# The triangular inverse of a Gated-DeltaNet layer: one stretch of products per doubling step instead of two

## The chip, the cores and the metric

The kernel runs on one core of a Trainium2 chip. The metric is the device time of one launch in microseconds, taken as the median of several runs. Four compute engines matter here: PE (TensorE, the matrix array), DVE (VectorE), ACT (ScalarE) and POOL (GpSimd). SP's queue issues the loads from HBM.

## The reference, cut to what matters

The program is a two-layer trunk for 512 tokens of width 1024. Each layer has a mixer and a gated MLP with a short convolution. Layer 0 mixes by four mLSTM heads and four Gated-DeltaNet heads; layer 1 by HGRN2. The change is in the Gated DeltaNet:

```python
def gated_delta_chunkwise(q, k, v, g, beta):
    ...
    kk = jnp.einsum("nbhld,nbhsd->nbhls", kc, kc)
    a_mat = jnp.where(strict, bc[..., :, None] * kk * decay, 0.0) + jnp.eye(L)
    rhs = jnp.concatenate([vc * bc[..., None], kc * (bc * jnp.exp(G))[..., None]], -1)
    sol = lax.linalg.triangular_solve(a_mat, rhs, left_side=True, lower=True, unit_diagonal=True)
    u, w = sol[..., :DV], sol[..., DV:]
```

Every chunk of every head needs the inverse of a unit lower triangular matrix, I plus a strictly lower part. Everything is float32.

## The kernel before, in words

**Tiles.** The kernel takes chunks of P = 128 tokens, so the 512 tokens are NT = 4 chunks. The four Gated-DeltaNet heads are done two at a time: `gdn_pair` is called once for pair 0 and once for pair 1, and each call has PC = 8 matrices of 128x128 to invert (two heads, `a` = 0 and 1, of four chunks). The matrix sits transposed and negated in `mt`, made on DVE from products of k with itself and the decay `dec`.

**The inverse.** A 128x128 matrix is cut in two diagonal blocks of 64 rows, one in partitions 0 to 63 (`lo`) and one in 64 to 127 (`hi`). For the 16 such blocks of a pair, the kernel keeps the inverse X of the block diagonal part found so far and its transpose, in tiles `X` and `xt` of 128 partitions x 8 x 64. They begin as identities (`units`). The step of level b (2, 4, 8, 16, 32) doubles the size of the blocks from b to 2b:
- 16 products `pp` = X times M (L1184), each 64x64, into one PSUM bank;
- ACT copies that bank to SBUF, into `PR` (L1186);
- 16 products `pe` (L1190) and 16 `pet` (L1191), which multiply `PR` by X from the other side, as they are and transposed, into two banks;
- on DVE, `fill` (L1100, a copy_predicated) takes from `pe` what the mask of the level lets through into `X`, and the same from `pet` into `xt`, with the masks `masks` and `maskst`.

Level 1 needs no product but a turn of the matrix into place (`pp` at L1155 and `pq` at L1156), and the end joins the two 64-row blocks (L1197, L1200, L1205) and has ACT copy the result into `mt` (L1209, L1210). Between the levels the program has the products of k and q (`at`, ahead of level 2), the transposes of q (`qt`, ahead of level 8, whose squares ACT sums into `nq`) and of v (`vt`, ahead of levels 16 and 32).

**What stands around it.** The weights are split into a high and a low part: ACT casts a loaded weight to `whi` (L228), and DVE or POOL subtracts to get `wlo` (L99). A projection of 128x512 is then three products (L127, `uh`/`ul` with `whi`/`wlo`), named `pf` for the short convolution's inputs and `pt` for a 256 columns wide one. Such products are independent of the inverse, and they are set between its stretches on PE. The convolution itself is a row of `scalar_tensor_tensor` on DVE (L102), and its silu is on ACT. `gdn(0)`, `mlstm(0)`, `gdn(1)` and `mlstm(1)` are written in this order, and a scheduler interleaves their instructions by the tiles that they need; `issue_after` pins one instruction behind another. What comes out is one order for each engine, in which the engine waits at each instruction until its inputs are there.

**PSUM.** Eight banks: three for projections, two (`mxt`) that the products of the inverse take in turn, two named "sc", one named "po".

Of the kernel before, what the change touches and what calls it, by code (L numbers as in the profile page):

```python
# [18 lines left out]
P = 128  # L19
# [15 lines left out]
def kernel(  # L35
# [741 lines left out]
    def ab_mix(pm, u, x0, g0):  # L777
# [7 lines left out]
        def small(name, shape, bufs=1, dt=F32):  # L785
            return pm.tile(shape, dt, tag=name, name=name, bufs=bufs)
# [27 lines left out]
        then(A.activation, out=one, in_=one, func=AF.Sqrt)  # L814
        unit = [units(then)]

# [150 lines left out]
        mk = small("masks", [P, 5, 64 // 4], dt=I32)  # L967
        mkt = small("maskst", [P, 6, 32 // 4], dt=I32)
        for i, hf in enumerate((slice(0, 64), slice(64, P))):
            nc.sync.dma_start(  # L970
                out=mk[hf],
                in_=block_masks[hf, P // 4 : 6 * P // 4].rearrange("p (l n) -> p l n", l=5)[:, :, i * 16 : (i + 1) * 16],
            )
            for j in range(len(RADIX4)):
                at = (6 + 3 * j) * P // 4
                nc.sync.dma_start(
                    out=mkt[hf, 2 * j : 2 * j + 2],
                    in_=block_masks[hf, at : at + P // 2].rearrange("p (l n) -> p l n", l=2)[:, :, i * 8 : (i + 1) * 8],
                )
        mk, mkt = mk.bitcast(U8), mkt.bitcast(U8)  # L980
        th = small("th", [P, NT, 8])
# [105 lines left out]

        def fill(b, x_, data, t):

            def part(ap):  # L1090
                return ap.rearrange("p c (n a r) -> p c n a r", a=2, r=b)[:, :, :, t, :]

            if t:
                mask = mkt[:, LEVELS.index(b), :].rearrange("p (n r) -> p n r", r=b)
            elif b == 1:
# [3 lines left out]
            mask = mask.unsqueeze(1).broadcast_to([P, PC, 32 // b, b])  # L1099
            V.copy_predicated(out=part(x_), mask=mask, data=part(data))  # L1100

        def gdn_pair(j, k, q, vf, gates):
            heads = (2 * j, 2 * j + 1)
            decs, qds, kbes, kds, pts = ([None, None] for _ in range(5))
            gl = small("gl", [P, 2, NT], bufs=2)
            ss = col(8, "l2s")
            for a, h in enumerate(heads):
# [11 lines left out]
                tt(V, v4(kd), v4(pt), bc(v4(dec)[:, :, P - 1], P), ALU.mult)  # L1119
                decs[a], qds[a], kbes[a], kds[a] = dec, qd, kbe, kd  # L1120
            v = col(8, "l2v")
# [12 lines left out]
                beta[:, :, heads[0] : heads[1] + 1].rearrange("p c a -> p a c"), ALU.mult,  # L1134
            )
            mts = []
            for a in range(2):
                dm = s("sig")
                stt(v4(dm), v4(decs[a]), -1.0, bc(dr[:, a], P), ALU.mult, ALU.mult)
# [10 lines left out]

            xt, xx = unit.pop() if unit else units()
            pp, pq = (chunks(mxt(n)) for n in ("pp", "pq"))
            for c in range(PC):
                for rs, cs, os in both:
                    T.matmul(pp[rs, c], lhsT=mc[c][rs, cs], rhs=identc[rs], start=True, stop=True)  # L1155
                    T.matmul(pq[os, c], lhsT=identc[rs], rhs=mc[c][rs, cs], start=True, stop=True)  # L1156
            fill(1, xx, pp, 0)
            fill(1, xt, pq, 1)
            for a in range(2):
                pa = mxt("at")  # L1160
                for cs in css:
                    T.matmul(pa[:, cs], lhsT=k[a][:, cs], rhs=q[a][:, cs], start=True, stop=True)
                tt(V, decs[a], pa, decs[a], ALU.mult)
            nq = col(8, "nq")
            vbs = []
            for b in LEVELS[1:-1]:
                if b == 8:
                    for a in range(2):
                        pt = mxt("qt")
                        transpose4(pt, q[a], range(NT))  # L1170
                        chunk_squares(nq[:, 4 * a : 4 * a + 4], v4(pt))

                    V.tensor_scalar(out=nq, in0=nq, scalar1=EPS, scalar2=0.5 * P * EPS, op0=ALU.add, op1=ALU.mult)
                if b > 8:
                    a = len(vbs)
                    pt = mxt("vt")
                    transpose4(pt, vf[a], range(NT))
                    vb = s("v")
                    tt(V, v4(vb), v4(pt), bc(ik[:, 4 * a : 4 * a + 4], P), ALU.mult)
                    vbs.append(vb)  # L1180
                pp = chunks(mxt("pp"))
                for c in range(PC):
                    for rs, cs, os in both:
                        T.matmul(pp[os, c], lhsT=mc[c][rs, cs], rhs=xx[rs, c], start=True, stop=True)  # L1184
                pr = small("PR", [P, PC, 64])
                A.copy(out=pr, in_=pp)  # L1186
                pes = [chunks(mxt(n)) for n in ("pe", "pet")]
                for c in range(PC):
                    for rs, _, os in both:
                        T.matmul(pes[0][rs, c], lhsT=xt[os, c], rhs=pr[os, c], start=True, stop=True)  # L1190
                        T.matmul(pes[1][os, c], lhsT=pr[os, c], rhs=xt[os, c], start=True, stop=True)  # L1191
                fill(b, xx, pes[0], 0)
                fill(b, xt, pes[1], 1)

            pp, pq = (chunks(mxt(n)) for n in ("pp", "pq"))
            for c in range(PC):
                T.matmul(pp[lo, c], lhsT=mc[c][lo, hi], rhs=xx[lo, c], start=True, stop=True)  # L1197
            for c in range(PC):
                for rs, _, os in both:
                    T.matmul(pq[rs, c], lhsT=identc[os], rhs=xt[os, c], start=True, stop=True)  # L1200
            pr = small("PR", [P, PC, 64])
            A.copy(out=pr[lo], in_=pp[lo])
            pd = chunks(mxt("pd"))
            for c in range(PC):
                T.matmul(pd[lo, c], lhsT=pr[lo, c], rhs=xt[lo, c], start=True, stop=True)  # L1205
            for a in range(2):
                ac = slice(a * NT, (a + 1) * NT)
                for rs, cs, _ in both:
                    A.copy(out=v4(mts[a])[rs, :, cs], in_=pq[rs, ac])  # L1209
                A.copy(out=v4(mts[a])[lo, :, hi], in_=pd[lo, ac])  # L1210
            gss = gates()
# [531 lines left out]
```

## Time and profile before

| | |
|---|---|
| three runs | 1333.91, 1331.79, 1333.54 us |
| median | 1333.54 us |
| the profiled execution, its own time | 1332.16 us |
| its span, first instruction to last | 1330.5 us |
| PE busy, mean granted clock | 1311.6 us (99%), 0.999 |
| PE weight loads busy | 1092.6 us (82%) |
| DVE / ACT / POOL busy | 659.4 (50%) / 612.5 (46%) / 364.6 (27%) us |
| moved by DMA | 121.23 MB, 91 GB/s in the mean |

A line of a group gives the source line, the engine, the operation, the output tile and its inputs, the count, the busy time, the mean of one in ns, and the idle time of the engine ahead of it. A line of the timeline gives the start in us, the duration in us, the engine and the operation, and in brackets the time for which the engine waited ahead of it and on what. A line of windows gives the stretch of time, its length, then for PE, PEld, DVE, ACT and POOL the busy time and the instructions, then the granted clock, the share of DMA and GB/s. A line of waits gives who waited on whom: the sum, the count and the longest, in us. Products overlap in the array, so that a product's duration is longer than its distance to the next one; the price of a product is read from the distance.

### The profile page before, as it was taken

How to read it: one execution, taken by the hardware profiler on the slowest of the kernel's cores; microseconds unless marked ns; L12 is line 12 of the kernel's file. 1: busy time of each engine (PE TensorE's matmuls, PEld its weight loads, DVE VectorE, ACT ScalarE, POOL GpSimd, SP SyncE). 2: the span in 40 equal slices, each digit the busy share in tenths (PEclk: the TensorE clock that was granted, in tenths of full speed). 3: DMA queues.
4: the chain of work that ended last, by engine and by line, in shares of the span. 5: the costliest groups of instructions: out<-in, count | busy, mean ns of one | idle time of the engine just before them, and what ended most of it. 6: DMA issues, size and time to landing. Idle time of an engine off the chain costs nothing.

```text
span 1330.5 us, 20034 instructions
## 1 busy us (share of the span) xinstructions
PE 1311.6 (99%) x7933; PEld 1092.6 (82%) x7933; DVE 659.4 (50%) x1287; ACT 612.5 (46%) x1168; POOL 364.6 (27%) x195
## 2 busy tenths in 40 slices
PE   8999999999999999999999999999999999999998
PEld 8788887879888888888888888887898888888886
DVE  6863774467533333311276783976764333331114
ACT  6654663554543333333346654564554333333222
POOL 1000000000755555544200000000055555554440
PEclk9999999999999999999999999999999999999999
DMA  6621131151533333222305122231243333322211
GB/s 175 167 64 38 48 94 37 47 173 59 150 95 95 96 95 98 103 96 100 111 17 149 58 80 80 68 108 33 80 127 111 95 96 95 95 95 96 98 61 63
DMA packets 165563, 121.23 MB, mean 91 GB/s; under 512 B 9246, under 2 KB 151006, under 8 KB 165470
## 3 DMA queue, kind: packets, MB, share of 16 engines
q1 hardware_dynamic: 165470, 119.96, 29.6%
q8 instruction: 62, 1.02, 0.3%
q14 instruction: 31, 0.25, 0.1%
HBM read 117.85 MB, written 2.10 MB: 90 GB/s over the span
## 4 chain that ended last, share of the span: by engine, by line
PE 78%; ACT 2%; DVE 2%; DMA 1%; issue 0%; DVEq 0%; ACTq 0%
PE pf L127 43%; PE dn L127 15%; PE mo L124 4%; PE dn L124 3%; PE pf L124 3%; PE mo L127 2%; PE pt L127 2%; PE lev L1452 1%; PE pt L124 1%; PE ut L124 1%; DMA raw<-in_c_w_in_dram 1%; PE o L1520 1%; DVE wlo L99 1%; PE S L1519 1%; ACT whi L228 0%
## 5 line engine op out<-in xcount | busy, mean ns | idle before, releaser
L99 POOL TENSOR_TENSOR wlo<-raw,whi 128x1024 fp32r<-128x1024 f32 x122 | 294.6, 2416 | 595.8 <-ACT whi L228 589.7
L127 PE MATMUL pf<-ul,whi 128*128 128x512 f32 x1040 | 408.5, 393 | 0.0
L127 PE MATMUL pf<-uh,whi 128*128 128x512 f32 x1040 | 407.4, 392 | 0.0
L127 PE MATMUL pf<-uh,wlo 128*128 128x512 f32 x1040 | 407.0, 391 | 0.0
L228 ACT CAST whi<-raw 128x1024 fp32r<-128x1024 f32 x192 | 201.1, 1051 | 218.7 <-PE pf L127 204.4
L102 DVE SCALAR_TENSOR_TENSOR acc<-pf,fcw,acc 128x511 f32<-128x511 f32 (+1 forms) x176 | 131.8, 749 | 274.2 <-ACT acc L306 271.1
L127 PEld LDWEIGHTS pf<-ul,whi 128*128 128x128 f32 x1040 | 195.3, 188 | 40.0
L127 PEld LDWEIGHTS pf<-uh,wlo 128*128 128x128 f32 x1040 | 195.3, 188 | 39.7
L127 PEld LDWEIGHTS pf<-uh,whi 128*128 128x128 f32 x1040 | 195.3, 188 | 39.6 <-issue 0.2
L127 PE MATMUL dn<-whi,hh 128*128 128x512 f32 x288 | 112.2, 390 | 0.0
L99 DVE TENSOR_TENSOR hl<-h,hh 128x512 fp32r<-128x512 f32 x44 | 32.0, 728 | 161.7 <-ACT hh L589 161.7
L127 PE MATMUL dn<-whi,hl 128*128 128x512 f32 x288 | 112.1, 389 | 0.0
L127 PE MATMUL dn<-wlo,hh 128*128 128x512 f32 x288 | 112.0, 389 | 0.0
L99 DVE TENSOR_TENSOR wlo<-raw,whi 128x1024 fp32r<-128x1024 f32 x70 | 85.2, 1222 | 40.7 <-ACT whi L228 38.3
L589 ACT CAST hh<-h 128x512 fp32r<-128x512 f32 x44 | 27.4, 623 | 155.2 <-PE dn L127 131.5
L1063 POOL TENSOR_SCALAR_AFFINE_SELECT dec<-dec 128x512 f32<-128x512 f32 x8 | 7.3, 911 | 244.3 <-DVE dec L99 179.1
L306 ACT ACTIVATE acc<-pf,fcb,fcw 128x512 f32<-128x512 f32 x88 | 68.2, 775 | 4.2 <-PE pf L124 3.2
L99 POOL TENSOR_TENSOR sg<-sg,acc 128x512 f32<-128x512 f32 x44 | 57.9, 1315 | 25.5 <-ACT sg L565 25.2
L127 PEld LDWEIGHTS dn<-whi,hh 128*128 128x128 f32 x288 | 54.1, 188 | 11.7 <-issue 0.5
L127 PEld LDWEIGHTS dn<-whi,hl 128*128 128x128 f32 x288 | 54.1, 188 | 11.2
L127 PEld LDWEIGHTS dn<-wlo,hh 128*128 128x128 f32 x288 | 54.1, 188 | 11.1
L565 ACT ACTIVATE sg<-acc 128x512 f32<-128x512 f32 x44 | 27.8, 632 | 68.2 <-DVE acc L102 68.2
(378 smaller groups left out, 1855.7 us busy)
## 6 DMA issues: line engine op xcount, KB each, us to landing
raw<-in_ffn_w_up_dram SPq DMA_DIRECT2D x88, 512.0 KB, 3.7
raw<-in_ffn_w_down_dram SPq DMA_DIRECT2D x44, 512.0 KB, 3.1
raw<-in_c_w_in_dram SPq DMA_DIRECT2D x32, 512.0 KB, 4.6
raw<-in_ab_w_in_dram SPq DMA_DIRECT2D x26, 512.0 KB, 3.7
gain<-in_norm_gains_dram SPq DMA_DIRECT2D x8, 512.0 KB, 4.3
raw<-in_ab_w_out_dram SPq DMA_DIRECT2D x8, 512.0 KB, 3.8
raw<-in_c_w_out_dram SPq DMA_DIRECT2D x8, 512.0 KB, 3.9
x<-in_x_dram SPq DMA_DIRECT2D x4, 512.0 KB, 6.0
```

The costliest lines, as they stand in the source:

```text
L99: return eng.tensor_tensor(out=o, in0=a, in1=b, op=op)
L102: return V.scalar_tensor_tensor(out=o, in0=a, scalar=s, in1=b, op0=op0, op1=op1, **kw)
L124: last[eng] = f(**kw)
L127: f(**kw)
L228: A.copy(out=hv, in_=rv)
L306: A.activation(out=acc, in_=ps, func=AF.Identity, scale=taps[:, K - 1 : K], bias=bias)
L565: A.activation(out=sg, in_=ag, func=AF.Sigmoid)
L589: A.copy(out=hi, in_=hT[k])
L1063: G.affine_select(out=v4(d), in_=v4(d), pattern=[[0, NT], [1, P]], compare_op=ALU.is_ge, fill=-BIG, base=0, channel_multiplier=-1,)
L1452: e = T.matmul(pls[a][i * 64 : (i + 1) * 64, c], lhsT=krs[a][:, c * P + i * 64 : c * P + (i + 1) * 64], rhs=qfs[a][:, :, at : at + 32], st ...
L1519: T.matmul(pS[:, :P], lhsT=kt[:, cs], rhs=vc, start=True, stop=True)
L1520: T.matmul(po[:, cs], lhsT=at[:, cs], rhs=vc, start=True, stop=c == 0)
```

## The change

The step no longer carries X and its transpose. It carries a factor X and Z = N X, N being the strictly triangular part, transposed as it lies. With B the part that the level's mask lets through, taken from the product, both are multiplied by I + B:
- `turned` (L1180): 16 products bring the matrix into place for level 1, in one bank for each head.
- Per level 1, 2, 4, 8, 16, 32, `fill` (L1097) takes B from the product into a factor `e`, head by head (128x128 each). ACT copies Z of each head from PSUM into `PR` (L1192, 128x256, from level 2 on). DVE then empties the other factor of the level before with a fill from `zeros`. Two factors, `xt` and `X`, take turns, and they hold identities apart from B.
- `doubled`, one stretch for each level: 16 products for the new Z (L1210) and 16 for the product that holds the next B (L1212; eight at the last level), into one bank for each head. All 32 need only `e` and Z, so nothing comes between them.
- The second head's halves trade places: `both[hf ^ (a & i)]` and `both[hf ^ (a & (i + 1))]` write the second head's result for rows 0 to 63 into partitions 64 to 127 and the other way round, at alternate levels, while the first head's stay.
- At the end DVE adds the identity to both halves (six `tensor_tensor`), 8 products `pp` (L1226), an ACT copy, 8 products `pd` (L1230), and two ACT copies into `mt`.
- The products `at`, the transposes `qt` with the squares for `nq`, and the transposes `vt` now come ahead of the levels, in the banks "sc" (`qt` and `at` ahead of `mt`, `vt` behind level 1's fill).
- The strict triangle is now taken by POOL: an affine_select makes `dm` from `dec`, once a head. The masks `maskst` and their six loads on SP's queue go away; `zeros` is a new small tile, cleared by POOL.

```diff
+            for a in range(2):
+                pa = bank("sc", "at")
+                ...
+            nq = col(8, "nq")
+            for a in range(2):
+                pt = bank("sc", "qt")
+                ...
-            pp, pq = (chunks(mxt(n)) for n in ("pp", "pq"))
+            pzs, zt = [of_head(mxt("pz")) for _ in range(2)], None
+            def turned(c, a, hf):
+                rs = both[hf][0]
+                return T.matmul(pzs[a][rs, 0, c], lhsT=mc[a * NT + c][rs, rs], rhs=identc[rs], start=True, stop=True)
+            in_a_row(turned, [(c, a, hf) for c in range(NT) for a in (1, 0) for hf in range(2)])
+            for i, b in enumerate(LEVELS[:-1]):
+                e = factors[i % 2]
+                if b > 1:
+                    zt = small("PR", [P, PC, 64])
+                for a in range(2):
+                    ac = slice(a * NT, (a + 1) * NT)
+                    filled = fill(b, e[:, ac], pzs[a][:, 0])
+                    if b > 1:
+                        A.copy(out=zt[:, ac], in_=pzs[a][:, 1])
+                if b > 1:
+                    fill(b // 2, factors[1 - i % 2])
+                ...
+                pzs = [of_head(mxt("pz")) for _ in range(2)]
+                def doubled(w, c, a, hf):
+                    rs, os = both[hf ^ (a & i)][0], both[hf ^ (a & (i + 1))][0]
+                    ac = a * NT + c
+                    z = mc[ac][rs, rs] if zt is None else zt[rs, ac]
+                    if w:
+                        return T.matmul(pzs[a][os, 1, c], lhsT=e[rs, ac], rhs=z, start=True, stop=True)
+                    if b < 32 or not hf:
+                        return T.matmul(pzs[a][os, 0, c], lhsT=z, rhs=e[rs, ac], start=True, stop=True)
+                in_a_row(doubled, [(w, c, a, hf) for w in (1, 0) for c in range(NT) for a in (1, 0) for hf in range(2)])
-            for b in LEVELS[1:-1]:
-                ...
-                pp = chunks(mxt("pp"))
-                for c in range(PC):
-                    for rs, cs, os in both:
-                        T.matmul(pp[os, c], lhsT=mc[c][rs, cs], rhs=xx[rs, c], start=True, stop=True)
-                pr = small("PR", [P, PC, 64])
-                A.copy(out=pr, in_=pp)
-                pes = [chunks(mxt(n)) for n in ("pe", "pet")]
-                for c in range(PC):
-                    for rs, _, os in both:
-                        T.matmul(pes[0][rs, c], lhsT=xt[os, c], rhs=pr[os, c], start=True, stop=True)
-                        T.matmul(pes[1][os, c], lhsT=pr[os, c], rhs=xt[os, c], start=True, stop=True)
-                fill(b, xx, pes[0], 0)
-                fill(b, xt, pes[1], 1)
+            xx = small("PR", [P, PC, 64])
+            for a in range(2):
+                tt(V, xx[lo, a * NT : (a + 1) * NT], pzs[a][lo, 0], bm(identc[lo], NT), ALU.add)
+            for rs in (hi, lo):
+                for a in range(2):
+                    tt(V, v4(mts[a])[rs, :, rs], pzs[a][rs, 1], bm(identc[rs], NT), ALU.add)
+            ...
             for c in range(PC):
-                T.matmul(pd[lo, c], lhsT=pr[lo, c], rhs=xt[lo, c], start=True, stop=True)
+                T.matmul(pd[lo, c], lhsT=xx[hi, c], rhs=mc[c][hi, hi], start=True, stop=True)
```

The instructions of PE in pair 0, in the kernel before, from the products `at` to the first products of level 2's second half:

```order
L1162 MATMUL at<-q,k 128x128 x8
L1184 MATMUL pp<-X,mt 64x64 x16
L127 MATMUL pf<-ul,whi 128x512
L127 MATMUL pf<-uh,wlo 128x512
L127 MATMUL pf<-uh,whi 128x512
L127 MATMUL pf<-ul,whi 128x512
L1190 MATMUL pe<-PR,xt 64x64
L1191 MATMUL pet<-xt,PR 64x64
L1190 MATMUL pe<-PR,xt 64x64
L1191 MATMUL pet<-xt,PR 64x64
```

The same place in the changed kernel, from the turn to the end of level 2's stretch (`pz` is the product's bank; `PR` in it is Z):

```order
L1180 MATMUL pz<-identc,mt 64x64 x16
L127 MATMUL pf<-uh,whi 128x512
L127 MATMUL pf<-ul,whi 128x512
L1210 MATMUL pz<-mt,xt 64x64 x16
L1212 MATMUL pz<-xt,mt 64x64 x16
L127 MATMUL pf<-uh,wlo 128x512
L127 MATMUL pf<-uh,whi 128x512
L127 MATMUL pf<-ul,whi 128x512
L127 MATMUL pf<-uh,wlo 128x512
L1210 MATMUL pz<-PR,X 64x64 x16
L1212 MATMUL pz<-X,PR 64x64 x16
```

A level had two stretches with projections between them and has one; `at` has moved ahead of the turn, and between stretches stand two `pf`, then four (further on 8, 4, 4 and 4). In pair 1 they are `pt`: 3, 7, 6, 6, 6, 6, and 19 behind the last level.

On DVE in pair 0 before, the fills of levels 2 and 4 and what follows them (`wlo` is the weight split, `q` a convolution step):

```order
L1100 COPY_PREDICATED X<-masks,pe 128x128x2
L1100 COPY_PREDICATED xt<-maskst,pet 128x128x2
L1100 COPY_PREDICATED X<-masks,pe 128x64x4
L1100 COPY_PREDICATED xt<-maskst,pet 128x64x4
L99 TENSOR_TENSOR wlo<-raw,whi 128x1024
L102 SCALAR_TENSOR_TENSOR q<-pf,cmix,q 128x511
L102 SCALAR_TENSOR_TENSOR q<-pf,cmix,q 128x510
L102 SCALAR_TENSOR_TENSOR q<-pf,cmix,q 128x509
L1173 TENSOR_SCALAR nq<-nq 128x8
```

And in the changed kernel, from level 1's `vt` on through levels 2, 4 and 8:

```order
L99 TENSOR_TENSOR v<-vt,ik 128x512 x2
L1097 COPY_PREDICATED X<-masks,pz 128x64x2 x2
L1097 COPY_PREDICATED xt<-mk_119,zeros 128x256
L99 TENSOR_TENSOR wlo<-raw,whi 128x1024
L102 SCALAR_TENSOR_TENSOR k<-pf,cmix,k 128x511
L1097 COPY_PREDICATED xt<-masks,pz 128x32x4 x2
L1097 COPY_PREDICATED X<-masks,zeros 128x128x2
L102 SCALAR_TENSOR_TENSOR k<-pf,cmix,k 128x510
L102 SCALAR_TENSOR_TENSOR k<-pf,cmix,k 128x509
L1097 COPY_PREDICATED X<-masks,pz 128x16x8 x2
```

The weight split and a convolution step now stand between level 2's and level 4's fills, and two more steps ahead of level 8's. The operation for `nq` has moved out, to ahead of those that make `mt`.

On DVE in pair 1 before, levels 1, 2 and 4:

```order
L1100 COPY_PREDICATED X<-mk_119,pp 128x256
L1100 COPY_PREDICATED xt<-maskst,pq 128x256
L99 TENSOR_TENSOR dec<-at,dec 128x512 x2
L99 TENSOR_TENSOR wlo<-raw,whi 128x1024
L1100 COPY_PREDICATED X<-masks,pe 128x128x2
L1100 COPY_PREDICATED xt<-maskst,pet 128x128x2
L99 TENSOR_TENSOR wlo<-raw,whi 128x1024
L1100 COPY_PREDICATED X<-masks,pe 128x64x4
L1100 COPY_PREDICATED xt<-maskst,pet 128x64x4
```

And in the changed kernel:

```order
L99 TENSOR_TENSOR wlo<-raw,whi 128x1024
L1097 COPY_PREDICATED xt<-mk_119,pz 128x128 x2
L99 TENSOR_TENSOR v<-vt,ik 128x512 x2
L1097 COPY_PREDICATED X<-masks,pz 128x64x2 x2
L1097 COPY_PREDICATED xt<-mk_119,zeros 128x256
L1097 COPY_PREDICATED xt<-masks,pz 128x32x4 x2
L1097 COPY_PREDICATED X<-masks,zeros 128x128x2
L1097 COPY_PREDICATED X<-masks,pz 128x16x8 x2
```

The weight splits that stood between the fills of pair 1 stand ahead of them. On POOL the four `sig<-dec` selects and the clearing of `zeros` are new, and on SP's queue six mask loads are gone.

More of the change, by code (lines that the diff above doesn't have):

```diff
@@ L814, in ab_mix @@
         then(A.activation, out=one, in_=one, func=AF.Sqrt)
-        unit = [units(then)]
+        factors = units(then)
+        zeros = small("zeros", [P, 32])
+        G.memset(zeros, 0.0)
         kparts = ((0, 3), (3, 6), (6, 8))
@@ L967, in ab_mix @@
         mk = small("masks", [P, 5, 64 // 4], dt=I32)
-        mkt = small("maskst", [P, 6, 32 // 4], dt=I32)
         for i, hf in enumerate((slice(0, 64), slice(64, P))):
@@ L973, in ab_mix @@
             )
[L974 to L980, printed above, removed]
+        mk = mk.bitcast(U8)
         th = small("th", [P, NT, 8])
@@ L1098, in fill, with in_a_row @@
                 mask = mk[:, LEVELS.index(b) - 1, :].rearrange("p (n a r) -> p n a r", a=2, r=b)[:, :, 0, :]
-            mask = mask.unsqueeze(1).broadcast_to([P, PC, 32 // b, b])
-            V.copy_predicated(out=part(x_), mask=mask, data=part(data))
+            shape = [P, x_.shape[1], 32 // b, b]
+            return V.copy_predicated(
+                out=part(x_), mask=mask.unsqueeze(1).broadcast_to(shape),
+                data=zeros.rearrange("p (n r) -> p n r", r=b).unsqueeze(1).broadcast_to(shape) if data is None else part(data),
+            )
+        def in_a_row(f, order):
+            with tc.issue_after(f(*order[0]).ins):
+                for what in order[1:]:
+                    f(*what)
         def gdn_pair(j, k, q, vf, gates):
             heads = (2 * j, 2 * j + 1)
-            decs, qds, kbes, kds, pts = ([None, None] for _ in range(5))
+            decs, qds, kbes, kds, dms = ([None, None] for _ in range(5))
             gl = small("gl", [P, 2, NT], bufs=2)
@@ L1195, in gdn_pair @@
[L1195 to L1202, printed above, removed]
+            pzs, zt = [of_head(mxt("pz")) for _ in range(2)], None
@@ new lines, in gdn_pair @@
+            xx = small("PR", [P, PC, 64])
+            for a in range(2):
+                tt(V, xx[lo, a * NT : (a + 1) * NT], pzs[a][lo, 0], bm(identc[lo], NT), ALU.add)
+            for rs in (hi, lo):
+                for a in range(2):
+                    tt(V, v4(mts[a])[rs, :, rs], pzs[a][rs, 1], bm(identc[rs], NT), ALU.add)
+            if j == 0:
+                fill(32, e)
+            pp = chunks(mxt("pp"))
+            for c in range(PC):
+                T.matmul(pp[hi, c], lhsT=mc[c][lo, hi], rhs=xx[lo, c], start=True, stop=True)
@@ L1203, in gdn_pair @@
+            A.copy(out=xx[hi], in_=pp[hi])
             pd = chunks(mxt("pd"))
             for c in range(PC):
-                T.matmul(pd[lo, c], lhsT=pr[lo, c], rhs=xt[lo, c], start=True, stop=True)
+                T.matmul(pd[lo, c], lhsT=xx[hi, c], rhs=mc[c][hi, hi], start=True, stop=True)
             for a in range(2):
[L1207 to L1210, printed above, removed]
+                A.copy(out=v4(mts[a])[lo, :, hi], in_=pd[lo, a * NT : (a + 1) * NT])
```

61 lines of the change are left out of this document (27 added, 34 removed).

## The prediction

> **What bounds the kernel now.** I read the page's busy table and chain first, then the windows of the two stretches the change rewrites (a pair of Gated-DeltaNet heads each), then their timelines, then the waits.
>
> ```profile
> span 1330.5 us, 20034 instructions
> PE 1311.6 (99%) x7933; PEld 1092.6 (82%) x7933; DVE 659.4 (50%) x1287; ACT 612.5 (46%) x1168; POOL 364.6 (27%) x195
> PE 78%; ACT 2%; DVE 2%; DMA 1%; issue 0%; DVEq 0%; ACTq 0%
> ...
> 87.30:121.20 33.90, 33.20 (x690) 26.44 (x689) 17.07 (x28) 12.87 (x35) 0.00 (x0) 1.00 0.18 50
> 202.30:238.30 36.00, 33.39 (x700) 27.14 (x699) 14.80 (x25) 13.24 (x36) 0.00 (x0) 1.00 0.15 46
> ```
>
> PE is the bound of the whole program and of both windows (33.2 of 33.9 us, 33.4 of 36.0); DVE and ACT are under half busy there, DMA at 0.18 and 0.15. PE is busy only because projection products (`pf`, `pt`) are set between the steps of the inverse. A projection product done there is not done elsewhere, so the time changes by what the inverse takes of PE: its own products, the seams, and the waits left uncovered.
>
> ```profile
> 92.06 1.15 PE L1184 MATMUL pp<-X,mt 64*64 64x64 f32 x32
> 93.14 0.50 PE L127 MATMUL pf<-ul,whi 128*128 128x512 f32 x1
> 93.48 0.39 PE L127 MATMUL pf<-uh,wlo 128*128 128x512 f32 x1
> ...
> 93.94 0.40 PE L127 MATMUL pf<-ul,whi 128*128 128x512 f32 x1
> 94.27 0.27 PE L1190 MATMUL pe<-PR,xt 64*64 64x64 f32 x1
> ...
> 95.36 0.50 PE L127 MATMUL pf<-uh,wlo 128*128 128x512 f32 x1
> ```
>
> This is one level of pair 0, in order of time. The 16 `pp` products (32 records; two per product) hold PE from 92.06 to 93.14, 1.08 us; the 32 products `pe` and `pet` from 94.27 to 95.36, 1.09 us. Twice as many in the same time: `pp` uses two quadrants of the array, `pe` and `pet` all four. Between the stretches stand four `pf`, one each 0.23 us (93.48 to 93.94 is two), but the first takes 0.34 and the last 0.33 to the next small product: a stretch costs 0.2 us of seams beside its products.
>
> **The products.** First and last stretch of pair 0:
>
> ```profile
> 87.59 0.65 PE L1155 MATMUL pp<-identc,mt 64*64 64x64 f32 x14 [0.17 <-DVE mt L99]
> 89.17 0.50 PE L127 MATMUL pf<-ul,whi 128*128 128x512 f32 x1
> ...
> 117.02 0.97 PE L1197 MATMUL pp<-X,mt 64*64 64x64 f32 x13 [0.18 <-DVE X L1100]
> 117.95 0.98 PE L1200 MATMUL pq<-xt,identc 64*64 64x64 f32 x27
> 119.96 0.50 PE L127 MATMUL pf<-uh,wlo 128*128 128x512 f32 x1
> ```
>
> Before, a pair takes 1.58 (87.59 to 89.17) + 5 x (1.08 + 1.09) + 2.94 (117.02 to 119.96) = 15.4 us for 304 products. After: the turn, 16 products in two quadrants like `pp`, 1.08; six steps of up to 32 products in four quadrants, 6 x 1.09 (the last has 24, but eight of them in two quadrants, so it gains nothing); then 8 `pp` and 8 `pd`, each in one quadrant. For those: the 13 records of `pp` at L1197 start over 0.97 - 0.22, 0.06 us apart, so 16 take about 1.0 us, 1.07 with the hand-over. Sum 1.08 + 6.54 + 2.14 = 9.8 us for 216 products. Gain 5.6 us a pair, **11.2 us** in all. Seams: 12 stretches become 9, 3 x 0.2 a pair, **1.2 us**.
>
> The four-quadrant price rests on this: 32 products `pe` and `pet`, two in each half of the array at a time, take 1.09 us, 0.034 apiece; and `pq` at L1200, whose two halves alternate between the row halves and write one bank, gives 27 records in 0.98 us, 0.03 apart, half of one quadrant's 0.06.
>
> The new order writes one bank from both row halves twice running, then the other bank twice; before, `pe` and `pet` take turns by bank. So I price a step at four quadrants, and two row halves taking turns at one bank is the first rival. A rule speaks against this: the Trainium skill, "TensorEngine Tiling (Array Packing)", Restrictions and Gotchas, says that different row tiles cannot access the same PSUM bank at the same time. By it a step would go two at a time and take twice the price. The `pq` row, 27 records in 0.98 us, does not agree with it.
>
> **Waits that go.** On PE in the two windows:
>
> ```profile
> PE pp L1184 <- DVE X L1100: 0.9, 1, 0.9
> PE qt L238 <- DVE X L1100: 0.9, 1, 0.9
> PE pp L1197 <- DVE X L1100: 0.7, 2, 0.6
> ...
> PE wt L1217 <- ACT mt L1210: 0.3, 1, 0.3
> ...
> PE pp L1155 <- DVE mt L99: 0.2, 1, 0.2
> PE at L1162 <- DVE X L1100: 0.2, 1, 0.2
> ...
> 215.39 1.23 DVE L99 TENSOR_TENSOR wlo<-raw,whi 128x1024 fp32r<-128x1024 f32 x1 [2.87 <-ACT whi L228]
> 216.54 0.42 DVE L1100 COPY_PREDICATED X<-masks,pe 128x256 f32<-128x256 uint8 x1
> ...
> 217.01 1.09 PE L238 MATMUL qt<-ident,q 128*128 128x128 f32 x8 [0.85 <-DVE X L1100]
> ```
>
> **3.2 us**, nearly all in pair 1, where a weight split (`wlo`, 1.23 us on DVE) stands ahead of a fill. The new DVE queue of pair 1 has no split between the fills. I count all 3.2 as gone and price what comes instead.
>
> **Waits that come.** The new step is one chain: PE ends, DVE fills one head's half, then the other's, ACT copies Z of each head after that head's fill, PE starts when the second copy is done. Nearest rows:
>
> ```profile
> 106.64 0.50 PE L127 MATMUL pf<-uh,whi 128*128 128x512 f32 x1
> 106.76 0.43 DVE L1100 COPY_PREDICATED X<-masks,pe 128x256 f32<-128x256 uint8 x1 [1.66 <-PE pet L1191]
> ...
> 95.48 0.73 DVE L1100 COPY_PREDICATED X<-masks,pe 128x256 f32<-128x256 uint8 x1 [0.69 <-PE pet L1191]
> ...
> 113.66 0.50 PE L127 MATMUL pf<-ul,whi 128*128 128x512 f32 x1
> 113.83 0.59 ACT L1186 COPY PR<-pp 128x512 f32<-128x512 f32 x1 [4.03 <-PE pp L1184]
> 114.31 1.05 ACT L228 CAST whi<-raw 128x1024 fp32r<-128x1024 f32 x1
> ...
> 119.26 1.50 ACT L1209 COPY mt<-pq 64x256 f32<-64x256 f32 x4
> ...
> 123.83 0.29 DVE L1239 COPY gS<-S 128x128 f32<-128x128 f32 x1 [6.53 <-PE S L1230]
> ...
> 208.36 0.38 PE L127 MATMUL pt<-whi,uh 128*128 128x256 f32 x1
> 208.59 0.28 PE L127 MATMUL pt<-wlo,uh 128*128 128x256 f32 x1
> ...
> 102.56 2.31 DVE L102 SCALAR_TENSOR_TENSOR q<-pf,cmix,q 128x511 f32<-128x511 f32 x3
> ...
> 104.12 0.28 ACT L754 ACTIVATE junk<-qt 128x128 bf16<-128x128 f32 x1
> ...
> 104.52 0.28 ACT L754 ACTIVATE junk<-qt 128x128 bf16<-128x128 f32 x1
> ```
>
> DVE starts 0.12 after the next PE stretch has begun (106.64, 106.76). A fill of 128x256 takes 0.43, and 0.73 for the two finest levels (95.48); half of it I put at 0.30 (the 128x128 copy's 0.29) and 0.45, between 0.29 and the full 0.73. ACT copies 256 columns in 0.37 (four in 1.50; the bound above is 0.59). Hand-overs DVE to ACT and on to PE I take as 0.06 each; the row shown has 0.05 (DVE free of `X` at 216.96, PE at 217.01). From level 4 on the chain needs 0.12 + 0.30 + 0.06 + 0.37 + 0.37 + 0.06 = 1.28; at level 2, 1.43; at level 1, which has no copy, 0.12 + 2 x 0.40 + 0.06 = 1.0. The order says what covers it. Pair 0: 2 `pf` (0.67), 4 `pf` (1.13), 8 `pf`, then 4 three times. Pair 1 has `pt` at 0.12 each: 3 (0.57), 7 (1.05), 6 four times (0.93).
> - Pair 1: 0.43 + 0.38 + 4 x 0.35 = 2.2 us.
> - Pair 0, levels 1, 2, 16 and 32: 0.33 + 0.3 + 2 x 0.15 = 0.9.
> - Pair 0, level 4: behind the copies ACT has a weight cast (1.05), DVE that weight's split (1.23) and a convolution step (2.31 / 3 = 0.77) ahead of the fill. Cast, split, step, fill and two copies are about 4.0 us after the last copies; PE has 1.1 of products and 2.0 of `pf`: 0.85 left.
> - Pair 0, level 8: two more convolution steps on DVE, then a silu on ACT ahead of the copies: 0.6.
> - Ahead of the turn: the transposes of q and v now come before the inverse and wait for their bank until ACT has squared q (eight at 0.4, from 104.12 to 104.52), and the DVE op for `nq`, waiting for those squares, stands ahead of the ops that make `mt`. In pair 0 the chain ends about where PE arrives: 0.4; in pair 1 PE arrives some 3 us earlier than before: 0.7.
>
> Sum **5.6 us**. The bounds are 0 (the fillers suffice) and about 10 (every fill and copy at the price of the full tile: some 0.45 more at each of ten gaps).
>
> Priced at nothing: the zero fills (DVE, while PE multiplies, 1.09 us); the six adds at the end, 6 x 0.30 as half tiles, beside ten `pf` or nineteen `pt`, 2.3 us, of which only the first two adds stand ahead of the next products; the four extra POOL selects (0.91 us each by the row below; POOL has nothing to do in either window; cover gone, one delays `mt` by that much); the six mask loads less on SP's queue, far ahead of use.
>
> ```profile
> L1063 POOL TENSOR_SCALAR_AFFINE_SELECT dec<-dec 128x512 f32<-128x512 f32 x8 | 7.3, 911 | 244.3 <-DVE dec L99 179.1
> ```
>
> **Sum.** -11.2 - 1.2 - 3.2 + 5.6 = -10.0 us. The profiled execution took 1332.16 us (span 1330.5 and 1.7 around it), so 1322.2; it lies 1.4 under the median of the runs, 1333.54, so **1323.5 us**, 0.75% faster.
>
> **Rivals.**
> - One bank, one row half at a time (the other side). Each of 12 steps and both turns then takes twice its 1.09: 14 x 1.09 = 15 us, 1338.5, slower. It decides from 0.7 us more per stretch. The `pq` row speaks against it; the exact order of four has no row. 5%. The rule of the Trainium skill named above would give this time.
> - The chain is dearer: fills and copies at the full tile's price, 4.5 us more: 1328. For it: no row has a predicated copy of this size. 20%.
> - The fillers suffice, as PE comes later than I think: 1318 to 1320. For it: most waits are 0.4 or less. 12%.
> - The freed time is not got back: projections reach their weights sooner and wait there; 1332 to 1334. Against it: DMA at 0.15 to 0.18, ACT with 20 of 34 us free. 4%.
>
> **Chances.** Forecast 59%. What a measurement of this kernel can tell is 0.2%, 2.7 us. The likeliest case with the second and third rivals gives 91% faster; I take off 2 for what I have not seen: faster 0.89, same 0.06, slower 0.05. The range holds the forecast and those two rivals: 1318 to 1329.
>
> **What the profile would show.** Each of the two groups of products in the steps overlapping the other, a full step 1.1 us to the next `pf`; PE instructions fewer by 2 x 2 x 88 = 352, so 7581; PE waits on ACT's copies in ten gaps, 0.15 to 0.4 each, and a larger one at pair 0's level 4; no wait on a fill behind a split in pair 1. Steps of 2.2 us, or waits near 1 us in every gap, would make this wrong.

## The result and the profile after

The changed kernel takes 1320.37 us (four runs, 1320.03 to 1320.49) against 1333.72 of the kernel before on the same chip (four runs, 1331.79 to 1333.93): ratio 0.9904, 95% interval 0.989 to 0.9918. Timed again, beside the last experiments, it took 1321.38 against 1332.23, ratio 0.992 (0.9907 to 0.9934). The forecast was 1323.5, range 1318 to 1329. The profiled execution took 1320.03 us, 12.1 less than that of before, where the sum gave 10.0 less.

The page, and the windows of the two stretches from the turn to the product `wt`:

```profile
span 1318.3 us, 19346 instructions
PE 1302.2 (99%) x7581; PEld 1084.3 (82%) x7581; DVE 662.6 (50%) x1310; ACT 603.8 (46%) x1164; POOL 368.5 (28%) x200
```

```profile
87.10:110.00 22.90, 22.21 (x476) 17.17 (x476) 15.55 (x34) 8.15 (x18) 0.00 (x0) 1.00 0.13 34
194.20:215.30 21.10, 20.71 (x499) 18.70 (x497) 10.06 (x26) 5.43 (x19) 0.00 (x0) 1.00 0.10 28
```

PE is still 99% busy, with 7581 records, as forecast. The stretches are 22.9 and 21.1 us long where they were 33.9 and 36.0, but fewer projections and no `at`, `qt` or `vt` lie in them. With those taken out at their prices (0.231 a `pf`, 0.119 a `pt`, 0.1035 a record of `at`, `qt` or `vt`), pair 0 goes from 19.3 to 13.0 us and pair 1, up to its first `wt`, from 21.7 to 13.5: 14.6 us less. The rest of the program gave 2.5 back.

One gap and step of pair 0, in order of time, with DVE, ACT and PE:

```profile
98.90 0.50 PE L127 MATMUL pf<-uh,whi 128*128 128x512 f32 x1
98.94 0.50 DVE L1097 COPY_PREDICATED xt<-masks,pz 128x128 f32<-128x128 uint8 x2 [1.68 <-PE pz L1212]
99.34 0.65 ACT L1192 COPY PR<-pz 128x256 f32<-128x256 f32 x2 [1.57 <-DVE xt L1097]
...
99.70 0.39 PE L127 MATMUL pf<-uh,whi 128*128 128x512 f32 x1
100.02 0.70 PE L1210 MATMUL pz<-PR,xt 64*64 64x64 f32 x32
100.54 0.66 PE L1212 MATMUL pz<-xt,PR 64*64 64x64 f32 x32
101.12 0.50 PE L127 MATMUL pf<-ul,whi 128*128 128x512 f32 x1
```

The step's 32 products (64 records) hold PE from 100.02 to 101.12, 1.10 us: four quadrants at once, as priced. The chain ahead of it is the forecast one, somewhat shorter: DVE starts 0.04 after PE's next stretch, two fills take 0.50, ACT starts 0.40 into them and is done at 99.99, PE starts at 100.02. That is 1.12 us, against 1.28 forecast, and four `pf` cover it.

A step of pair 1, where the cover is short:

```profile
202.64 0.65 ACT L1192 COPY PR<-pz 128x256 f32<-128x256 f32 x2 [1.98 <-DVE X L1097]
...
203.07 0.83 PE L1210 MATMUL pz<-PR,X 64*64 64x64 f32 x26
...
203.81 0.81 PE L1212 MATMUL pz<-X,PR 64*64 64x64 f32 x28
204.56 0.39 PE L127 MATMUL pt<-whi,uh 128*128 128x256 f32 x1
```

PE starts at 203.07, while ACT copies until 203.29: one head's Z is there, the other's is not. Among the single records of the trace, the weight load that waits for the second copy comes at 203.34, and no product starts between 203.29 and then. The step is 1.49 us long, and part of that is a wait, though the busy time hides it: no row of PE's waits names it. The row of PE's weight loads names ACT's copies ahead of eight of the ten steps that need one:

```profile
PEld pz L1210 <- ACT PR L1192: 3.7, 8, 1.0
```

During part of these 3.7 us PE still works on projections, so they are not what the steps lose. Over the twelve steps, from the first product to the next projection, PE took 1.20, 1.19, 1.09, 1.35, 1.10, 1.16 in pair 0 and 1.32, 1.34, 1.11, 1.49, 1.35, 1.31 in pair 1, 15.0 us against 12 x 1.09 = 13.1.

What the waits on PE name in the changed kernel, from the view of all waits:

```profile
PE yt L238 <- DVE yn L99: 1.3, 3, 0.8
...
PE pz L1210 <- ACT PR L1192: 0.6, 1, 0.6
PE pt L127 <- issue: 0.4, 1, 0.4
...
PE mt L1166 <- ACT qd L1116: 0.3, 1, 0.3
...
PE vt L238 <- ACT junk L754: 0.2, 1, 0.2
```

The waits on fills behind weight splits are gone. The 0.6 is the forecast one at pair 0's level 4 (0.85 forecast). New and not forecast: `yt`, which waited 0.3 before.

One more gain lies where the change was thought to do nothing, 40 us ahead of the first turn. These are SP's queue, ACT and PE, first of the kernel before:

```profile
22.21 1.91 SPq L976 DMA_DIRECT2D maskst<-in_block_masks_dram  x3
...
24.81 1.92 SPq L976 DMA_DIRECT2D maskst<-in_block_masks_dram  x3
...
30.76 2.20 SPq L127 DMA_DIRECT2D raw<-in_ab_w_in_dram  x3
...
36.58 1.05 ACT L228 CAST whi<-raw 128x1024 fp32r<-128x1024 f32 x1 [1.49 <-DMA raw<-in_ab_w_in_dram]
...
47.73 0.38 PE L1012 MATMUL cum<-lsg,tri 128*128 128x32 f32 x2 [1.25 <-DVE lsg L99]
```

and of the changed kernel:

```profile
26.73 4.16 SPq L127 DMA_DIRECT2D raw<-in_ab_w_in_dram  x3
...
34.99 1.04 ACT L228 CAST whi<-raw 128x1024 fp32r<-128x1024 f32 x1
...
46.52 0.38 PE L1007 MATMUL cum<-lsg,tri 128*128 128x32 f32 x2
```

Six mask loads took 3.8 us of SP's queue ahead of three weight loads. Without them the weights are asked for 4 us earlier, the cast does not wait, DVE's `lsg` is in time and PE's 1.25 us are gone. Whether the loads are the cause is what the first two experiments ask.

### The profile page after: what moved, and what is told of

The parts are those of the page before. It is cut to its first block, busy times and chain, and to the rows that moved or that the text cites. A ratio compares the mean times of both kernels' runs of the same rounds, so it can differ in the third digit from the quotient of the medians.

```text
span 1318.3 us, 19346 instructions
## 1 busy us (share of the span) xinstructions
PE 1302.2 (99%) x7581; PEld 1084.3 (82%) x7581; DVE 662.6 (50%) x1310; ACT 603.8 (46%) x1164; POOL 368.5 (28%) x200
## 4 chain that ended last, share of the span: by engine, by line
PE 90%; ACT 4%; DVE 3%; DMA 1%; issue 1%; POOL 0%; SPq 0%; DVEq 0%; ACTq 0%; POOLq 0%
PE pf L127 49%; PE dn L127 15%; PE mo L124 4%; PE dn L124 3%; PE pf L124 3%; PE pt L127 2%; PE pt L124 2%; PE mo L127 2%; PE lev L1474 1%; PE ut L124 1%; ACT junk L754 1%; DMA raw<-in_ab_w_in_dram 1%; DVE wlo L99 1%; ACT whi L228 1%; DMA raw<-in_c_w_in_dram 1%
## 5 line engine op out<-in xcount | busy, mean ns | idle before, releaser
L127 PEld LDWEIGHTS dn<-whi,hh 128*128 128x128 f32 x288 | 54.1, 188 | 11.6 <-issue 0.5
L127 PEld LDWEIGHTS dn<-wlo,hh 128*128 128x128 f32 x288 | 54.1, 188 | 11.3
L127 PEld LDWEIGHTS dn<-whi,hl 128*128 128x128 f32 x288 | 54.1, 188 | 11.2
```

The costliest lines, as they stand in the source:

```text
L127: f(**kw)
```

## The experiments

All ratios are to the kernel before on the same chip. The experiments ran on three chips, on which the kernel before took 1331.95, 1332.23 and 1333.21 us in the median, so that times of different chips can differ by about 1 us for that alone.

**The six loads put back into the changed kernel.**

```diff
+        mkt = small("maskst", [P, 6, 16 // 4], dt=I32)
         for i, hf in enumerate((slice(0, 64), slice(64, P))):
             ...
+            for j in range(len(RADIX4)):
+                at = (6 + 3 * j) * P // 4
+                nc.sync.dma_start(out=mkt[hf, 2 * j : 2 * j + 2], in_=block_masks[hf, at : at + P // 2]...[:, :, i * 8 : i * 8 + 4])
```

> The changed kernel with six mask loads put back on SP's queue where they were, each half as wide as before (16 bytes a row piece instead of 32), into a tile that nothing reads. Theory A: the changed kernel gains 1.2 us at 46 us because the weight load behind those six loads is issued some 4 us earlier, so the cast, the split and with them lsg on DVE are no longer late for the products cum. Then this kernel's time is about 1321.6, PE waits about 1.2 us for lsg ahead of cum, and everything behind it starts 1.2 us later than in the changed kernel. Rival B, that of the prediction: six loads that are needed much later cost nothing; the time stays at 1320.4 and the 1.2 us came from the DVE order.

Measured: 1321.94 us (1320.91 to 1322.9), ratio 0.9921 (0.9906 to 0.9936). The trace, SP, ACT and PE:

```profile
30.28 2.41 SPq L127 DMA_DIRECT2D raw<-in_ab_w_in_dram  x3
...
35.19 1.04 ACT L228 CAST whi<-raw 128x1024 fp32r<-128x1024 f32 x1
...
46.79 0.38 PE L1014 MATMUL cum<-lsg,tri 128*128 128x32 f32 x2
```

Inconclusive. The weights were asked for half a microsecond earlier than before (30.28 against 30.76), in this execution they landed in time, and `cum` did not wait. The time, 1.6 over the changed kernel's on its chip, is the one that A named, but not by A's path in this trace: the profiled execution is 1.25 over the changed kernel's, and there PE waits 0.8 us more for `un` ahead of `ut` (1.9 against 1.1) and 0.7 more on "issue" (1.1 against 0.4). The runs lie in two groups (1320.9 and 1321.3, 1322.6 and 1322.9) and the trace is of the lower one.

**The six loads behind the weights, in the kernel before.**

```diff
-            for j in range(len(RADIX4)):
-                nc.sync.dma_start(out=mkt[hf, 2 * j : 2 * j + 2], ...)
 ...
+            if j == 0:                       # in gdn, behind the loads of its weights
+                with tc.issue_after(loads[-1].ins):
+                    ... the same six loads
```

> The kernel before, with its six loads of maskst set behind the three weight loads on SP's queue instead of ahead of them; nothing else is moved. Theory A: the loads ahead hold the weight loads up for 3.8 us of SP's queue, so that the cast at 36.6 us waits 1.5 us for its weights and PE 1.25 us for lsg; set behind, both waits go and the time falls by 1.2 us to about 1330.8. Rival B, for which the run with the loads put back into the changed kernel speaks (no wait ahead of cum there): these 1.2 us belong to how the transfers fell in one execution, and the time stays within 0.5 us of the kernel before, 1332.

Measured: 1331.2 us against 1333.21, ratio 0.9987 (0.9978 to 0.9996): 0.5 to 2.9 us faster.

```profile
26.63 4.32 SPq L221 DMA_DIRECT2D raw<-in_ab_w_in_dram  x3
31.00 4.43 SPq L1343 DMA_DIRECT2D maskst<-in_block_masks_dram  x6
...
35.06 1.03 ACT L231 CAST whi<-raw 128x1024 fp32r<-128x1024 f32 x1
...
46.50 0.38 PE L1009 MATMUL cum<-lsg,tri 128*128 128x32 f32 x2
```

Theory A holds: all six loads are still there, and both waits are gone. What cost was their place in the queue. Part of the 2 us between the medians is not theirs: the kernel before had a mean granted clock of 0.997 in 11 of its 21 executions, this one in 3 of 11. Executions of the same mean clock (0.997, 0.998, 0.999) are 1.2, 1.7 and 1.0 us faster in the mean, which fits the 1.2 of the trace. This is a gain of the change that the inverse has no part in, and the old kernel could have had it alone. It is not there in every execution, as the run with the loads put back shows.

**Without the trading places.**

```diff
-                    rs, os = both[hf ^ (a & i)][0], both[hf ^ (a & (i + 1))][0]
+                    rs = os = both[hf][0]
```

> The changed kernel without the trading places: both heads' halves stay where they are, so that all 32 products of a step use the two quadrants on the diagonal. Theory A: a product holds its quadrant, 16 products in two quadrants take 1.08 us, so a full step takes 2.16 instead of 1.10 and the last one 1.6; 2 x (5 x 1.06 + 0.5) = 11.6 us more, about 1332, which is almost the whole gain of the change. Rival B: the gain is from one stretch in place of two, and the products overlap anyway; at most 2 us more, about 1322.

Measured: 1328.57 us, ratio 0.9974 (0.9964 to 0.9984). Its windows and one step:

```profile
87.30:114.30 27.00, 27.00 (x476) 22.22 (x476) 15.65 (x34) 8.27 (x18) 0.00 (x0) 1.00 0.11 27
198.60:223.70 25.10, 25.10 (x498) 23.34 (x497) 10.10 (x26) 5.43 (x19) 0.00 (x0) 1.00 0.08 24
```

```profile
99.49 1.15 PE L1210 MATMUL pz<-PR,X 64*64 64x64 f32 x32
100.47 1.10 PE L1212 MATMUL pz<-X,PR 64*64 64x64 f32 x32
101.50 0.50 PE L127 MATMUL pf<-uh,whi 128*128 128x512 f32 x1
```

A step takes 2.01 us instead of 1.10, and each stretch is 4.0 to 4.1 us longer (27.0 and 25.1 against 22.9 and 21.1), 8.1 in all; the time is 8.2 over the changed kernel's, and 8.0 over that of the next experiment, which ran on the same chip. Theory A holds in kind. It gave 11.6, since it set 2.16 against 1.10 a step; the trace has 24.6 us for the twelve steps against 15.0, and the waits at levels 4 and 8 and the "issue", 1.2 us, are gone with the longer steps. The trading places carry 8 of the 11.3 us that the kernel of the next experiment is under the kernel before on that chip.

**The order of the banks.**

```diff
-  [(w, c, a, hf) for w in (1, 0) for c in range(NT) for a in (1, 0) for hf in range(2)]
+  [(w, c, a, hf) for w in (1, 0) for c in range(NT) for hf in range(2) for a in (1, 0)]
```

> The changed kernel with the products of a step in another order: the two heads, and with them the two banks, take turns at every product instead of after every two. Theory A: the steps that take 1.2 to 1.5 us instead of 1.10 do so because their second head's Z is still being copied when the first head's products start; the order of the banks changes nothing: 1320.4 within 0.5, and steps of the same mixed lengths. Rival B: two products in a row into one bank from both row halves hold each other up; then all steps come down to 1.10, about 1318.5.

Measured: 1320.61 us, ratio 0.9911 (0.9896 to 0.9926), steps of 1.20, 1.28, 1.10, 1.35, 1.18, 1.18 and 1.31, 1.36, 1.10, 1.47, 1.24, 1.27. Theory A: the steps, which decide it, are as mixed as before, and the clean ones still take 1.10. Two products running into one bank, from the two row halves, hold nothing up.

**Z in banks of its own**, at every level, and then from level 2 on:

```diff
-                        A.copy(out=zt[:, ac], in_=pzs[a][:, 1])
+                        A.copy(out=zt[:, ac], in_=zs[a][:, 1])    # ahead of both fills
...
+                zs = pzs if b == 1 else [of_head(bank("sc", "pzz")) for _ in range(2)]
-                        return T.matmul(pzs[a][os, 1, c], lhsT=e[rs, ac], rhs=z, start=True, stop=True)
+                        return T.matmul(zs[a][os, 1, c], lhsT=e[rs, ac], rhs=z, start=True, stop=True)
```

The first had `bank("sc", "pzz")` at level 1 too.

> The changed kernel with Z written into the two banks named sc and the product for B into the two banks of the inverse, so that ACT can copy Z while PE still makes the second half of the step. Theory A: what is left of the chain is the fill alone (two of 0.25 us), and the fillers of 0.5 to 1.1 us cover it; steps all 1.10, no waits on ACT's copies; about 2 us less, 1318.4, with the 0.6 us at pair 0's level 4 partly left, since there a weight split and a convolution step stand ahead of the fill. Rival B: ACT's copies and the waits for the sc banks take it back, 1320.4 or more.

> The changed kernel with Z in the two sc banks from level 2 on, and as in the changed kernel at level 1, where the transposes of v hold the sc banks. Theory A: ACT's copies of Z run beside the second half of the products, so the steps that start before the second copy is done (1.2 to 1.5 us instead of 1.10) all come down to 1.10, which is 1.9 us over both pairs; with what is lost at pair 0's level 4 left, 1320.4 - 1.5 = 1318.9. Rival B: the sc banks are late for other work, or the fill ahead of each step, two of 0.25 us, is the last to end anyway; 1320.4 or more.

Measured: 1322.44 (ratio 0.9925, 0.9909 to 0.9942) and 1321.75 (0.9914, 0.99 to 0.9927). Rival B both times in the time, though not in the steps. Behind level 4 of pair 1 in the second kernel, DVE and ACT:

```profile
202.49 0.49 DVE L1097 COPY_PREDICATED X<-masks,pz 128x128 f32<-128x128 uint8 x2 [2.04 <-PE pz L1215]
202.60 0.65 ACT L1191 COPY PR<-pzz 128x256 f32<-128x256 f32 x2 [2.49 <-PE pz L1215]
```

ACT did not copy Z beside the second half of the products: it waited for the last product of the whole step, as the fill does (`<-PE pz L1215`). So the copies moved up by 0.3 us, no more, and the idea was not tested as meant. Even that much brought the steps down: from level 4 on all eight of the first kernel take 1.08 to 1.09 us, and six of eight of the second (the others 1.57 and 1.49). What the traces show against it stands at the early levels and at the end: waits for copies (0.8 us once in each) and for fills (0.5 and 0.3), "issue" (0.4 and 0.9), and `pp` at the end cut in two by a projection. No run took these apart.

**The moves alone, in the kernel before**: `at` and `qt` ahead of `mt`, `vt` behind level 1's fill, in the banks "sc", the triangle from POOL.

> The kernel before with only the moves of the change: at and qt ahead of mt, vt behind level 1's fill, in the banks sc, and the strict triangle from POOL; the inverse is that of before. Theory A: in the kernel before, at, qt and vt stand between the stretches and cost seams and waits there: 0.43 us four times behind vt, 0.3 twice behind at, 0.9 ahead of qt and 0.9 ahead of pp, 4.1 us; moved ahead they cost the 1.9 us that the changed kernel shows there, so about 2.2 us are gained, 1329.8, and the new inverse alone is worth some 9. Rival B: the waits on DVE's fills behind weight splits stay, since the order on DVE stays, and the moves bring nothing or cost up to 2 us: 1332 to 1334.

Measured: 1334.27 us against 1333.21, ratio 1.001 (1.0001 to 1.0019): 0.1 to 2.5 us slower. Rival B in its time, not for its reason. Waits on PE:

```profile
PE ut L124 <- DVE un L124: 2.0, 1, 2.0
PE cum L1012 <- DVE lsg L99: 1.5, 1, 1.5
...
PE yt L238 <- DVE yn L99: 1.1, 2, 0.8
...
PE pp L1201 <- DVE X L1100: 0.6, 1, 0.6
PE pp L1188 <- DVE X L1100: 0.3, 2, 0.2
```

The two waits of 0.9 behind weight splits are gone here too, with the old inverse: `pp` keeps 0.3 at the levels, and the 0.6 at the end (L1201). But `yt`'s 0.8 has come, as in the changed kernel, and so has the slower stretch ahead of the turn (0.6 and 1.5 us more in the two pairs, the moved products themselves taken out). So the moves take away the waits of 0.9 and cost as much elsewhere. (The 0.8 more at `ut` is not theirs: that wait lies between 0.6 and 2.0 us in all the traces.) The changed kernel is 11 to 13 us under the kernel before; with 1 us more for the moves and the loads' 1.2 to 2.0 apart, the new inverse alone is worth some 10 to 13, if the moves cost the same beside it, which no run shows.

**Copies twice.**

```diff
                         A.copy(out=zt[:, ac], in_=pzs[a][:, 1])
+                        A.copy(out=zt[:, ac], in_=pzs[a][:, 1])
```

> The changed kernel with each of ACT's copies of Z made twice (the second writes the same again). It puts two more copies, 0.65 us, into the chain of each of the ten gaps. Theory A: the fillers of 0.9 us and more just cover the chain of 1.1 us, so nearly all of it shows: 10 x 0.65 = 6.5 us less 0.5 for the two longer gaps, about 1326. Rival B: the fillers have room left and no more than 2 us show, 1322.5.

Measured: 1322.02 us, ratio 0.9917 (0.9903 to 0.9931): 0.6 to 1.7 more than the changed kernel's two medians, where theory A had 5.6. Rival B, and the trace shows how. PE and ACT ahead of level 2 of pair 0:

```profile
90.60 0.67 ACT L1192 COPY PR<-pz 128x256 f32<-128x256 f32 x2 [7.27 <-DVE X L1097]
91.16 0.66 ACT L1193 COPY PR<-pz 128x256 f32<-128x256 f32 x2
...
91.34 0.40 PE L127 MATMUL pf<-ul,whi 128*128 128x512 f32 x1
91.67 0.82 PE L1211 MATMUL pz<-PR,X 64*64 64x64 f32 x30
```

Six `pf` lie in this gap, which had four; all five gaps of pair 0 now hold six `pf`, and all five of pair 1 eleven `pt` where they held six or seven. So the scheduler sets projections between two steps by the length of the chain. A longer chain is paid for with fillers taken from elsewhere, which costs little as long as there are some.

**The transposes in the gaps.**

```diff
+                if b in (1, 2):
+                    pt = bank("sc", "qt")
+                    with tc.issue_after(step.ins):          # step: the level's last product
+                        transpose4(pt, q[a], range(NT))
+                ...
+                if b in (8, 16):
+                    pt = bank("sc", "vt")
+                    with tc.issue_after(step.ins):
+                        transpose4(pt, vf[a], range(NT))
```

> The changed kernel with the transposes of q pinned behind the steps of levels 1 and 2 and those of v behind the steps of levels 8 and 16, in the banks sc; at stays ahead of the inverse. On PE they then stand in the gaps between steps in place of projections (four transposes and one pf instead of four pf). Theory A: what the moves cost is the stretch ahead of the turn, where the changed kernel loses 1.9 us more than the kernel before; in the gaps the transposes cover the chain as well as projections do, so about 1.5 us are gained: 1319. Rival B: ACT's squares of q (four at 0.4 us) then stand ahead of its copies of Z at levels 2 and 4 and the steps wait for them, 1 to 2 us each: 1321 to 1324.

**The changed kernel again.**

> The changed kernel as it is, beside the others on the same chip. Theory A: 1320.0 to 1321.5, about 0.9% under the kernel before, and once more a stall of 0.4 to 0.9 us on PE in pair 1, near 201 us, for which nothing that the profile shows is to blame, as in every kernel with the new inverse so far. Rival B: that stall belongs to single executions and is absent here.

Measured: 1319.8 us for the transposes in the gaps (1319.56 to 1321.25; ratio 0.9909, 0.9896 to 0.9923), 1321.38 for the changed kernel beside it (1320.99 to 1322.57; 0.992, 0.9907 to 0.9934). That is 1.6 lower, as A had it, and the version is the fastest of all; but the intervals overlap, so that the difference is not settled. At the same mean granted clock (0.997, 0.998, 0.999) it is 0.8, 1.4 and 1.3 us lower, with one or two executions each. One gap of it:

```profile
101.27 0.66 PE L238 MATMUL vt<-ident,v 128*128 128x128 f32 x4
101.68 0.48 PE L127 MATMUL pf<-ul,whi 128*128 128x512 f32 x1
102.14 0.83 PE L1194 MATMUL pz<-PR,X 64*64 64x64 f32 x26
```

Four transposes and one `pf` fill a gap that held four `pf`, in 0.87 us instead of 1.13; the step behind them is 1.35 us long instead of 1.16, so gap and step together are about as long as before.

**`at`, `qt` and `vt` written between the levels**, nothing pinned.

> The changed kernel with at, qt and vt written between the levels, where the kernel before has them, but in the banks sc and with nothing pinned. The order that results still has them on PE ahead of the turn, since the banks sc are free early: only the fillers shift (seven pf instead of four behind level 1 of pair 0, four instead of eight behind level 2) and DVE's products with vt come ahead of mt. Theory A: where they are written does not matter, the banks do; within 1 us of the changed kernel. Rival B: the 0.6 us wait at pair 0's level 4 goes with the new fillers and DVE's queue is freer behind the turn; 1 us or more faster.

Measured: 1322.52 us (1320.6 to 1323.93), ratio 0.9924 (0.991 to 0.9937). Theory A as far as the spread of 3.3 us can tell; the last section shows two things that lengthened the profiled execution.

## Why the prediction was right, and where it was off

The direction and the mechanism held: PE is the bound, what the inverse takes of it is the price, four quadrants work at once, and fewer stretches have fewer seams. 1320.4 is 3.1 below the forecast and inside the range. That the difference of the profiled executions, 12.1, is no further from the 10.0 of the sum is in part luck: 3.9 us of gain that the sum did not have (1.4 in the waits at the steps, 1.3 and 1.2 in terms set to nothing) stand against 1.8 of cost. By its own terms, for the profiled executions:

| term | forecast | the runs |
|---|---|---|
| products, two pairs | -11.2 | turn 1.08, `pp` 1.07, `pd` 1.08, a clean step 1.09 to 1.10: as priced |
| seams, six fewer | -1.2 | 0.10 ahead of a stretch, 0.11 behind (88.28 to 88.62 us where two `pf` are 0.23 apart): as priced |
| waits that go | -3.2 | gone |
| waits that come, at the steps | +4.5 | 3.1: 1.9 inside the steps, 0.6 at level 4, 0.15 at level 8, 0.4 "issue" |
| ahead of the turn | +1.1 | 1.9 for all that was moved there (0.25 in pair 0, 1.66 in pair 1) |
| `at`, `qt`, `vt` leaving the levels | 0 | about -1.3: seams of 0.3 behind `at` and 0.12 behind each `vt`, and 0.3 ahead of one `at` |
| six loads off SP's queue | 0 | -1.2 in the trace; 0.5 to 2.9 by the run with them set later, 1.0 to 1.7 at the same mean clock |
| `yt` | 0 | +1.0 |

With the first three terms at their forecast the right column sums to the -12.1 measured, but not place by place: inside the two stretches the terms give -13.8 where the windows show -14.6, outside +1.7 where the difference is +2.5. So 0.8 us on either side is assigned to nothing. The table also leaves out `lev`, far behind the inverse, which waited 0.8 us and then 0.3: over all the traces that wait lies between 0.2 and 2.2, so it belongs to single executions.

**The term that failed** is "the six mask loads less on SP's queue, far ahead of use", priced at nothing. The loads' own use was far off, but the weights queued behind them were not: 3.8 us on SP made a cast, a split and a PE product late (`cum` waits 1.25 and 1.5 us in two traces with the loads ahead, and not at all in the third). The trace of before had the row `cum` <- `lsg`, 1.25 us; the waits were read in the two windows of the inverse only.

**The waits that come** were the right ones, with 1.12 for a chain of 1.28. Most do not appear as waits: PE starts on one head's Z and lags inside the step. "The fillers suffice", the rival at 1318 to 1320, is nearest in time to what came, but it did not happen: 3.1 of the 4.5 us forecast at the steps were there, and its reason, that PE comes later than thought, shows nowhere. The time came near it through the terms set to nothing.

**Ahead of the turn** and **`yt`** went the other way, 1.8 us more than priced. The moved work was priced by what waits at the turn; its seams, and `yt`, which waits 0.8 us behind pair 1 also when only the moves are made, were left out.

**One bank, one row half at a time** (1338.5) is refuted: steps of 1.10 us, and no change when the banks take turns. The Trainium skill, "PSUM — Partial Sum Buffer", section "PSUM bank collisions raise a hardware error", quotes the same rule, but what it reports as measured is narrower: row tiles collide when they write one bank and one quadrant (32 partitions) of it. The trace agrees as far as it goes: at every step a head's two row halves write one bank, each its own 64 partitions, and 32 products take 1.10 us; no run here wrote one quadrant from both.

## What to carry to other kernels

A load that is taken off a queue can be worth what stands behind it, not what its own data are worth: read the whole list of waits, not only those in the stretch that is rewritten. Where PE is the bound and projections can be set anywhere, price a rewritten chain by its products and seams first; a chain made longer by 0.65 us in ten gaps cost under 2 us in all. And products of 64x64 pay for themselves when all four quadrants have work: trading the halves of one head brought a step from 2.01 to 1.10 us and carried 8 of some 11 to 13 us.

## What the runs showed of the hardware that was not expected

In pair 1 PE stalls at about the same place, near 201 to 205 us, with no wait that the profile shows. Rows of the changed kernel, of its second timing and of the kernel written between:

```profile
200.83 0.28 PE L127 MATMUL pt<-whi,ul 128*128 128x256 f32 x1 [0.39 <-issue]
```

```profile
201.46 0.28 PE L127 MATMUL pt<-whi,ul 128*128 128x256 f32 x1 [0.68 <-issue]
```

```profile
202.79 0.34 PE L1213 MATMUL pz<-X,PR 64*64 64x64 f32 x7 [1.71 <-issue]
```

Among the kernels with the new inverse it was absent only where the transposes stand in the gaps and where the places are not traded (which the expectation of the second timing had overlooked); in the kernel before and its two variants it never showed. From one execution to another it varies, 0.39 and 0.68 in the same kernel, so it is part of the spread of their times.

The packets in the traces point at a cause. Besides data, the DMA engines move packets of the kind "instruction"; the page counts 60 of them in queue q8, and the packet records give each 16 KB. In the changed kernel the last one ahead of pair 1's turn comes at 177.66 us and the next at 198.55, 201.96, 205.39 and 209.15: 21 us apart, then 3.4 to 3.8, which fits PE's many small products there. A weight load of 512 KB moves from 196.2 to 198.6; the instruction packet starts as that load ends (198.55) and ends at 199.50, and PE goes on at 200.83. The same order stands in all eight traces with a stall: the packet starts within 0.3 us of the end of a weight load, and PE goes on 1.33 to 1.46 us after the packet's end (in the kernel with 1.71: packet 200.38 to 201.33, PE at 202.79). With the transposes in the gaps the load is over by 194.5, the packet comes at 196.65, and there is no stall. Without the trading places a packet also starts as a load ends (203.05), and PE does not stall, but there a step takes 2.01 us for the same products. So PE seems to run out of instructions that a load holds up; no run moved that load alone, so this is not shown.

A second part of the spread is the granted clock. In the second timing's trace it stands at 0.50 for 3.4 us from 917.3 on, far behind the inverse, and in the kernel written between from 203.5 to 206.9, behind the stall of 1.71. The same two microseconds, in the second timing and in the changed kernel's first trace (the figure of 0.50 or 1.00 is the clock):

```profile
918.00:920.00 2.00, 2.00 (x7) 1.62 (x6) 0.91 (x2) 0.87 (x2) 0.00 (x0) 0.50 0.00 0
```

```profile
918.00:920.00 2.00, 2.00 (x10) 1.37 (x9) 1.73 (x3) 2.00 (x5) 0.00 (x0) 1.00 0.00 0
```

At 0.50 a product of 128x512 follows the last after 0.43 us instead of 0.23. In both traces a wait of PE of 1.4 us (`mo` for `yhi`) stands just ahead; behind it the clock fell in one and not in the other. Of the kernel before on one chip, the 11 executions with a mean clock of 0.997 took 1333.7 us in the mean and the five with 0.999 took 1332.1.
